# Residual and embedding rows by fours, and an earlier multiplication by the norm's weights, in the last stage of a decoder layer

## Chip, cores and metric

One core of a Trainium2 chip runs the whole kernel. The metric is the device time of one execution in microseconds (us). Runs of one kernel scatter by some 0.1%, so a change of less than 0.2% (4.3 us) counts here as no change.

## What is computed

One decoder layer on a residual stream of 1024 tokens by 1024 channels, all float32: a half-step feed-forward, a token mixer, a second half-step feed-forward, and a last stage that adds a gated embedding. The change touches the last stage alone:

```
def _rmsnorm(x, g):
    xf = x.astype(jnp.float32)
    y = xf * lax.rsqrt(jnp.mean(xf * xf, axis=-1, keepdims=True) + EPS)
    return (y * g.astype(jnp.float32)).astype(x.dtype)
...
        gate = jax.nn.sigmoid(_rmsnorm(h, ple_pre_g[i]) @ ple_w_gate[i])
        e = p[i] @ ple_w_proj[i]
        h = h + _rmsnorm(gate * e, ple_post_g[i])
```

## The kernel before

Tokens lie on the 128 partitions, so the 1024 tokens are eight **token blocks** t = 0 to 7, each 128 x 1024, cut into two halves of 512 channels. Every large product is done by Strassen's scheme (Winograd's form): both operands are cut into 2 x 2 blocks of 512, seven products of sums of blocks are formed in the order p1, p2, p5, p6, p3, p7, p4 (`ORDER`), and the result's blocks are read as they become complete: block 11 (t 0 to 3, first half) after p2, block 12 (t 0 to 3, second half) after p3, block 22 (t 4 to 7, second half) after p7, block 21 (t 4 to 7, first half) after p4. So t 0 to 3 are complete after the fifth product, t 4 to 7 after the seventh. Float32 accuracy comes from splitting each operand into a high and a low part (`split`: a cast on ScalarE, L147, then a subtraction on VectorE, L148) and three matmuls per step (`mm3`, L155 to L157). In the last stage a product has 4 token blocks x 4 steps x 3 = 48 matmuls of 128 x 512.

The left operand is held by `Seven`: seven tiles from the pool `X` (seven buffers of 16 KB per partition), filled as the token blocks of the normalized stream are transposed on TensorE (L232): op 0 and op 1 for p1 and p2, later op 2 to op 6 for p5, p6, p3, p7, p4 (`sums`, L207 to L218; the tile `rest` holds two of its terms). The right operand, the weights `ple_w_gate`, is loaded by `Rows` (L522) into the pool `raw` (six buffers), summed there (L151), and split into the pool `wt` (four buffers). `closing` ends the stage before: for each token block it computes the residual (L730), writes it to memory as `h3` (L731), and normalizes it (L178) for the transposes. The pools `f` (`full`, eleven tiles of 4 KB per partition) and `hf` (`half`, four of 2 KB) hold the rest.

`ple_final` (L1169 ff.) is called for each token block and half as a block of the gate product completes. It loads the half row of the embedding `e` (L1178, 256 KB), takes the sigmoid of the product (ScalarE, L1179), multiplies by e (VectorE, L1180) and sums the squares (ScalarE, L168). GpSimd computes the scale r = (mean + eps)^-0.5 of the row (L174 for the half that comes first; L162 and L163 with the second). For the half that completes the row it then loads the residual row h3 (L1185, 512 KB) and, for both halves, multiplies by r and by the norm's weights (`scaled`, L178), adds the residual (L151) and stores the result (L1191). The weights themselves are loaded once, when the first block arrives (L182).

All these loads and stores are issued by SyncE (SP) on one queue. The order of instructions on each engine is not written by hand: the framework's scheduler sets it from the program, together with the small work queue `later`, and each engine then runs its list strictly in that order. A tile whose pool is full takes the buffer that comes free, and its first writer waits for the last reader there.

Of the kernel before, what the change touches and what calls it, by code (L numbers as in the profile page):

```python
# [13 lines left out]
P = 128  # L14
# [69 lines left out]
def layer_kernel(ctx: ExitStack, tc: tile.TileContext, a: dict, out: bass.AP):  # L84
# [24 lines left out]
    def raw(shape, dt=F32):  # L109

        return rawp.tile([P, *shape], dt, name="raw", tag="raw")
# [5 lines left out]
    def half():  # L117

        return hfp.tile([P, HT], F32, name="hf", tag="hf")
# [39 lines left out]
    def rsqrt(src, scale, offset=EPS):  # L159

        ms, r = scalar_tile(), scalar_tile()
        nc.gpsimd.tensor_scalar(ms, src, scale, offset, op0=ALU.mult, op1=ALU.add)  # L162
        nc.gpsimd.tensor_tensor(r, ms, nhalf, op=ALU.pow)  # L163
        return r

    def squares(src, junk):
        ss = scalar_tile()
        nc.scalar.activation(junk, src, AF.Square, accum_out=ss)  # L168
        return ss

    def mean_part(src, junk, scale, offset):

        out = scalar_tile()
        nc.gpsimd.tensor_scalar(out, squares(src, junk), scale, offset, op0=ALU.mult, op1=ALU.add)  # L174
        return out
# [4 lines left out]
    def gain(vec):  # L180
        g = full()
        nc.sync.dma_start(g, vec.partition_broadcast(P))  # L182
        return g
# [322 lines left out]
    class Rows:  # L506
# [27 lines left out]
            make = from_stored(block, put, sums) if stored else from_blocks(block, put)  # L534
            self.right = Right(lambda i: make(i, state, (False, False)), list(range(7)), 1)

        def run(self, left, outs, last):
            for i, (name, place, fresh) in enumerate(ORDER):
                if i == 6:
                    last()  # L540
                left.need(i)
                o = self.right.get(i)
                for t in range(4):
                    if i == 2:
                        later.flush(t + 6 if t < 3 else None)
                    s = left.op[i]
                    if fresh:
                        outs[t].b[place] = bank()
                    cols = slice(t * P, (t + 1) * P)
                    for k in range(4):  # L550
                        oh = o[k // 2]
                        mm3(
                            outs[t].b[place], (s[:, 0, k, cols], s[:, 1, k, cols]),
                            (oh[:, 0, k % 2, :], oh[:, 1, k % 2, :]), fresh and k == 0, k == 3,
                        )
                    outs[t].read(name)
                    later.allow(2.7)
# [606 lines left out]
    )  # L1164


    m, parts, gains = {}, {}, []

    def ple_final(t, half_, part):  # L1169
        if not gains:  # L1170
            gains.append(gain(a["ple_post_g"][0]))
        g_ple = gains[0]
        h = slice(half_ * HT, (half_ + 1) * HT)
        if t not in m:
            m[t] = full()
        mt = m[t]
        e = half()
        nc.sync.dma_start(e, e_d[t][:, h])  # L1178
        nc.scalar.activation(mt[:, h], part, AF.Sigmoid)  # L1179
        nc.vector.tensor_tensor(mt[:, h], mt[:, h], e, op=ALU.mult)  # L1180
        if half_ != (1 if t < 4 else 0):
            parts[t] = mean_part(mt[:, h], e, 1.0 / D, EPS)
            return
        hp = raw([D])
        nc.sync.dma_start(hp, h3_d[t])  # L1185
        r = rsqrt(squares(mt[:, h], e), 1.0 / D, parts[t])
        for j in range(2):
            hj = slice(j * HT, (j + 1) * HT)
            scaled(mt[:, hj], mt[:, hj], r, g_ple[:, hj])
            add(hp[:, hj], hp[:, hj], mt[:, hj])  # L1190
            nc.sync.dma_start(out[0, t * P:(t + 1) * P, hj], hp[:, hj])  # L1191

    ple_rows.run(left, token_out(ple_final, m), lambda: None)


# [27 lines left out]
```

## Time and profile before

| | us |
|---|---|
| median of 3 runs | 2148.37 (2146.13 to 2148.41) |
| the profiled execution | 2153.78 |
| its span, first to last instruction | 2151.7 |
| last matmul of the stage before ends | 2033.7 |
| last matmul of the last stage ends | 2133.7 |
| busy in the span: TensorE (PE), VectorE (DVE), ScalarE (ACT), GpSimd (POOL) | 2070.9, 1472.0, 939.9, 141.0 |

In the profile PE is the matmul side of TensorE and PEld its weight load; PEclk is the clock that was granted to TensorE as a share of full speed. Busy time counts instructions that run. In a timeline the start of each instruction is the sound number: durations are given a little long where one instruction follows another at once (a VectorE operation of 128 x 512 reads 0.68 and starts 0.60 after the one before).

### The profile page before, as it was taken

The numbers are of one execution on the slowest core, as the hardware profiler recorded it, in microseconds if no ns is written. First come the engines' busy times: TensorE is split into PE (matmuls) and PEld (weight loads), VectorE is DVE, ScalarE is ACT, GpSimd is POOL, SyncE is SP. The second block draws the span as 40 slices with busy tenths as digits, with TensorE's granted clock in tenths as the row PEclk, the third lists the DMA queues.
The fourth block names the chain that finished last, engine by engine and source line by source line (L and its number), as shares of the span: only waits on it lengthen the run. The fifth ranks groups of instructions, "written<-read, shape, count | busy, mean of one in ns | idle before, by whom it ended". The sixth has DMA issues, their size and how long they took to land. (4 is left out here: it accounts for less than half of the span.)

```text
span 2151.7 us, 25497 instructions
## 1 busy us (share of the span) xinstructions
PE 2070.9 (96%) x9228; PEld 1712.7 (80%) x9228; DVE 1472.0 (68%) x1773; ACT 939.9 (44%) x1360; POOL 141.0 (7%) x212
## 2 busy tenths in 40 slices
PE   7999999999999799999999999989999999999986
PEld 6888888888887688888787887778888888888765
DVE  6866666677566887567576758886666667545687
ACT  7533333344435543334455535643333334444553
POOL 2000000000021110000000002300000000002112
PEclk9999999999999899999999999999999999999988
DMA  8454545399768236445389986635454547764635
GB/s 287 128 171 157 176 142 184 129 340 384 298 221 320 69 100 193 158 142 177 128 282 340 324 233 204 195 112 188 146 186 136 172 149 272 231 197 175 225 118 195
DMA packets 301486, 429.52 MB, mean 200 GB/s; under 512 B 19888, under 2 KB 176560, under 8 KB 301360
## 3 DMA queue, kind: packets, MB, share of 16 engines
q1 hardware_dynamic: 300272, 425.80, 58.3%
q0 software_dynamic: 1088, 2.10, 0.6%
q8 instruction: 72, 1.18, 0.2%
q14 instruction: 54, 0.44, 0.1%
HBM read 290.72 MB, written 137.10 MB: 199 GB/s over the span
## 5 line engine op out<-in xcount | busy, mean ns | idle before, releaser
L155 PE MATMUL ps<-X,wt 128*128 128x512 f32 x1904 | 743.0, 391 | 4.1 <-DVE f L345 2.4
L156 PE MATMUL ps<-X,wt 128*128 128x512 f32 x1904 | 743.2, 390 | 0.9 <-DVE X L148 0.9
L157 PE MATMUL ps<-X,wt 128*128 128x512 f32 x1904 | 741.8, 390 | 0.0
L148 DVE TENSOR_TENSOR wt<-raw,wt 128x1024 fp32r<-128x1024 f32 x282 | 343.5, 1220 | 235.0 <-ACT wt L147 234.9
L155 PEld LDWEIGHTS ps<-X,wt 128*128 128x128 f32 x1904 | 359.3, 189 | 79.3 <-DVE f L345 2.8
L156 PEld LDWEIGHTS ps<-X,wt 128*128 128x128 f32 x1904 | 359.2, 189 | 76.0 <-DVE X L148 1.8
L157 PEld LDWEIGHTS ps<-X,wt 128*128 128x128 f32 x1904 | 358.8, 188 | 74.7
L147 ACT CAST wt<-raw 128x1024 fp32r<-128x1024 f32 x282 | 295.5, 1050 | 268.7 <-PE ps L157 129.2
L148 DVE TENSOR_TENSOR X<-raw,X 128x1024 fp32r<-128x1024 f32 (+1 forms) x201 | 224.0, 1145 | 113.6 <-ACT X L147 113.1
L147 ACT CAST X<-raw 128x1024 fp32r<-128x1024 f32 (+1 forms) x201 | 192.1, 993 | 156.2 <-PE ps L157 66.6
L156 PE MATMUL ps<-X 128*128 128x512 f32 x616 | 241.5, 392 | 0.3 <-DVE X L148 0.3
L155 PE MATMUL ps<-X 128*128 128x512 f32 x616 | 237.4, 391 | 3.7 <-ACT X L147 2.6
L157 PE MATMUL ps<-X 128*128 128x512 f32 x616 | 240.2, 391 | 0.0
L151 DVE TENSOR_TENSOR raw<-raw 128x1024 f32<-128x1024 f32 x136 | 165.8, 1221 | 15.4 <-DMA raw<-in_w_in_dram 5.5
L155 PEld LDWEIGHTS ps<-X 128*128 128x128 f32 x616 | 116.1, 189 | 28.6 <-ACT X L147 3.0
L156 PEld LDWEIGHTS ps<-X 128*128 128x128 f32 x616 | 116.4, 189 | 24.7 <-DVE X L148 0.8
L156 PE MATMUL ps<-wt,X 128*128 128x512 f32 x336 | 133.8, 398 | 1.8 <-DVE wt L148 1.8
L157 PEld LDWEIGHTS ps<-X 128*128 128x128 f32 x616 | 116.4, 189 | 24.0
L155 PE MATMUL ps<-wt,X 128*128 128x512 f32 x336 | 132.1, 401 | 1.2 <-DVE f L345 1.2
L157 PE MATMUL ps<-wt,X 128*128 128x512 f32 x336 | 133.0, 396 | 0.0
L340 ACT ACTIVATE f<-ps 128x512 f32<-128x512 f32 x88 | 52.6, 598 | 122.5 <-PE ps L157 122.3
L338 ACT ACTIVATE f<-ps 128x512 f32<-128x512 f32 x88 | 52.0, 597 | 109.4 <-PE ps L157 109.4
(136 smaller groups left out, 1856.9 us busy)
## 6 DMA issues: line engine op xcount, KB each, us to landing
raw<-ffn_s SPq DMA_DIRECT2D x70, 512.0 KB, 5.2
raw<-in_ffn_w_gate_dram SPq DMA_DIRECT2D x96, 256.0 KB, 3.4
raw<-in_ffn_w_up_dram SPq DMA_DIRECT2D x96, 256.0 KB, 4.1
f<-in_ffn_w_down_dram SPq DMA_DIRECT2D x44, 512.0 KB, 4.6
ffn_s<-hf SPq DMA_DIRECT2D x88, 256.0 KB, 3.4
ffn_t<-hf SPq DMA_DIRECT2D x88, 256.0 KB, 4.3
raw<-ffn_t SPq DMA_DIRECT2D x40, 512.0 KB, 5.2
ffn_s<-f SPq DMA_DIRECT2D x66, 256.0 KB, 2.1
```

The source lines that it names most:

```text
L147: nc.scalar.copy(hi, src)
L148: e.tensor_tensor(lo, src, hi.bitcast(F32), op=ALU.subtract)
L151: e.tensor_tensor(dst, u, v, op=ALU.add)
L155: nc.tensor.matmul(ps, wl[1], wr[0], start=first, stop=False, skip_group_check=True)
L156: nc.tensor.matmul(ps, wl[0], wr[1], start=False, stop=False, skip_group_check=True)
L157: nc.tensor.matmul(ps, wl[0], wr[0], start=False, stop=last, skip_group_check=True)
L338: nc.scalar.activation(at("22"), y, AF.Copy, scale=-1.0)
L340: nc.scalar.activation(at("12"), x, AF.Copy, scale=-1.0)
```

## The change

`ple_final` no longer loads anything. A function `beside`, called once per product from `Rows.run`, loads the norm's weights and all eight embedding rows (two `X` tiles of four rows each) ahead of p6, and the residual rows of t 0 to 3 ahead of p3 and of t 4 to 7 ahead of p7 (an `X` tile each). Each row is its own load of 512 KB. The sigmoid of block 11 is taken at once, and everything behind it is kept back in `gated_steps` until the rows are there. Behind the multiplication by e, the half row is multiplied in place by the norm's weights; when r is there, one operation per half row multiplies by r and adds the residual in its `X` tile, from where it is stored.

```
-        def run(self, left, outs, last):
+        def run(self, left, outs, last, beside=lambda i: None):
...
                 o = self.right.get(i)
+                beside(i)
                 for t in range(4):
...
-    m, parts, gains = {}, {}, []
+    m, parts, gains, e, h = {}, {}, [], {}, {}
+
+    def rows_of(src, dst, ts):
+        tile4 = X([4, D], F32)
+        for n, t in enumerate(ts):
+            dst[t] = tile4[:, n]
+            nc.sync.dma_start(dst[t], src[t])
+
+    def beside(i):
+        if i == 3:
+            gains.append(gain(a["ple_post_g"][0]))
+            rows_of(e_d, e, range(4))
+            rows_of(e_d, e, range(4, 8))
+        if i in (4, 5):
+            rows_of(h3_d, h, range(4 * i - 16, 4 * i - 12))
...
-        e = half()
-        nc.sync.dma_start(e, e_d[t][:, h])
-        nc.scalar.activation(mt[:, h], part, AF.Sigmoid)
-        nc.vector.tensor_tensor(mt[:, h], mt[:, h], e, op=ALU.mult)
-        if half_ != (1 if t < 4 else 0):
-            parts[t] = mean_part(mt[:, h], e, 1.0 / D, EPS)
-            return
-        hp = raw([D])
-        nc.sync.dma_start(hp, h3_d[t])
-        r = rsqrt(squares(mt[:, h], e), 1.0 / D, parts[t])
-        for j in range(2):
-            hj = slice(j * HT, (j + 1) * HT)
-            scaled(mt[:, hj], mt[:, hj], r, g_ple[:, hj])
-            add(hp[:, hj], hp[:, hj], mt[:, hj])
-            nc.sync.dma_start(out[0, t * P:(t + 1) * P, hj], hp[:, hj])
...
+        nc.scalar.activation(mt[:, cols], part, AF.Sigmoid)
+
+        def gated():
+            nc.vector.tensor_tensor(mt[:, cols], mt[:, cols], e[t][:, cols], op=ALU.mult)
+            if half_ != (1 if t < 4 else 0):
+                parts[t] = mean_part(mt[:, cols], half(), 1.0 / D, EPS)
+            else:
+                r = rsqrt(squares(mt[:, cols], half()), 1.0 / D, parts[t])
+            nc.vector.tensor_tensor(mt[:, cols], mt[:, cols], gains[0][:, cols], op=ALU.mult)
+            if half_ != (1 if t < 4 else 0):
+                return
+            for j in range(2):
+                hj = slice(j * HT, (j + 1) * HT)
+                nc.vector.scalar_tensor_tensor(h[t][:, hj], mt[:, hj], r, h[t][:, hj], op0=ALU.mult, op1=ALU.add)
+                nc.sync.dma_start(out[0, t * P:(t + 1) * P, hj], h[t][:, hj])
+
+        gated_steps.append(gated)
+        if e and (t >= 4 or half_ == 0 or len(h) > t):
+            while gated_steps:
+                gated_steps.pop(0)()
```

In the changed kernel the three VectorE lines are L1192 (times e), L1197 (times the norm's weights) and L1202 (times r, plus residual); the row loads are L1174, the stores L1203. Every engine's list is the same as before up to the start of the last stage. Three places behind it, as the lists stand (line, operation, output <- inputs with tile numbers, shape):

VectorE, start of the last stage, up to the normalization of token block 7 (`raw_15308`), which its transposes need. `X_15324` is `rest`; `X_15327`, `X_15330` are op 2 and op 6; `X_15630` is op 3 (in the change `X_15600`), `X_15708` is op 4; the `raw` sums with `raw_15557` are weights of p6 and p7. Before:

```order
L730 SCALAR_TENSOR_TENSOR f_14327<-f_14327,sc_15311,raw_15308 128x1024
L214 SCALAR_TENSOR_TENSOR f_14804<-f_14804,X_15324 128x512
L215 TENSOR_TENSOR f_14804<-f_14804,X_15324 128x512
L148 TENSOR_TENSOR X_15630<-X_15324,X_15630 128x4x128
L151 TENSOR_TENSOR raw_15435<-raw_15435,raw_15557 128x1024
L151 TENSOR_TENSOR f_15346<-f_15346,ps_15451 128x512
L151 TENSOR_TENSOR raw_15439<-raw_15439,raw_15557 128x1024
L151 TENSOR_TENSOR f_15370<-f_15370,ps_15475 128x512
L148 TENSOR_TENSOR X_15327<-X_15324,X_15327 128x4x128
L148 TENSOR_TENSOR X_15330<-ps_15424,X_15330 128x4x128
L148 TENSOR_TENSOR X_15708<-f_14804,X_15708 128x4x128
L178 SCALAR_TENSOR_TENSOR raw_15308<-f_14327,sc_15354,f_14075 128x1024
```

And now:

```order
L731 SCALAR_TENSOR_TENSOR f_14327<-f_14327,sc_15311,raw_15308 128x1024
L207 TENSOR_TENSOR X_15324<-ps_15424,X_15324 128x4x128
L214 SCALAR_TENSOR_TENSOR f_14804<-f_14804,X_15324 128x512
L215 TENSOR_TENSOR f_14804<-f_14804,X_15324 128x512
L148 TENSOR_TENSOR X_15600<-X_15324,X_15600 128x4x128
L151 TENSOR_TENSOR f_15346<-f_15346,ps_15451 128x512
L151 TENSOR_TENSOR f_15370<-f_15370,ps_15466 128x512
L148 TENSOR_TENSOR X_15327<-X_15324,X_15327 128x4x128
L178 SCALAR_TENSOR_TENSOR raw_15308<-f_14327,sc_15354,f_14075 128x1024
L148 TENSOR_TENSOR X_15330<-ps_15424,X_15330 128x4x128
```

The two weight sums, the op 4 part and the op 6 part now stand behind the normalization (L207, which stood ahead of L730, stands behind L731); two more parts of op 4 and op 5 that stood ahead of L730 have gone behind as well, because op 4 and op 5 now wait for buffers.

SP's queue, the same stretch. Before:

```order
L522 DMA raw_15441<-in_ple_w_gate_dram 128x2x512
L731 DMA h3_6_103<-f_14316 128x1024
L1178 DMA hf_15467<-e_0_105 128x512
L1178 DMA hf_15489<-e_1_106 128x512
L1178 DMA hf_15527<-e_2_107 128x512
L1178 DMA hf_15549<-e_3_108 128x512
L522 DMA raw_15557<-in_ple_w_gate_dram 128x2x512
L182 DMA f_15465<-in_ple_post_g_dram 128x1024
L731 DMA h3_7_104<-f_14327 128x1024
L522 DMA raw_15559<-in_ple_w_gate_dram 128x2x512
```

And now (three embedding rows, t 0 to 2, stand between `raw_15441` and the first row shown):

```order
L732 DMA h3_6_103<-f_14316 128x1024
L1174 DMA X_15628<-e_3_108 128x1024
L1174 DMA X_15633<-e_4_109 128x1024
L1174 DMA X_15633<-e_5_110 128x1024
L1174 DMA X_15633<-e_6_111 128x1024
L1174 DMA X_15633<-e_7_112 128x1024
L522 DMA raw_15527<-in_ple_w_gate_dram 128x2x512
L732 DMA h3_7_104<-f_14327 128x1024
L522 DMA raw_15529<-in_ple_w_gate_dram 128x2x512
```

All eight embedding rows now stand ahead of the weights of p6 (`raw_15527`, `raw_15529`; before `raw_15557`, `raw_15559`). Farther on, the residual rows of t 0 to 3 stand directly behind them, then p4's weights, then the norm's weights, then the residual rows of t 4 to 7, then all sixteen stores.

VectorE, the end of its list. Before:

```order
L178 SCALAR_TENSOR_TENSOR f_15582<-f_15582,sc_15975,f_15465 128x512 x2
L1180 TENSOR_TENSOR f_15627<-f_15627,hf_16056 128x512
L178 SCALAR_TENSOR_TENSOR f_15597<-f_15597,sc_16005,f_15465 128x512
L151 TENSOR_TENSOR raw_15970<-raw_15970,f_15582 128x512
L178 SCALAR_TENSOR_TENSOR f_15597<-f_15597,sc_16005,f_15465 128x512
L151 TENSOR_TENSOR raw_15970<-raw_15970,f_15582 128x512
L178 SCALAR_TENSOR_TENSOR f_15612<-f_15612,sc_16035,f_15465 128x512 x2
L151 TENSOR_TENSOR raw_16000<-raw_16000,f_15597 128x512
L178 SCALAR_TENSOR_TENSOR f_15627<-f_15627,sc_16065,f_15465 128x512 x2
L151 TENSOR_TENSOR raw_16000<-raw_16000,f_15597 128x512
L151 TENSOR_TENSOR raw_16030<-raw_16030,f_15612 128x512 x2
L151 TENSOR_TENSOR raw_16060<-raw_16060,f_15627 128x512 x2
```

And now:

```order
L1202 SCALAR_TENSOR_TENSOR X_15869<-f_15552,sc_15976,X_15869 128x512 x2
L1197 TENSOR_TENSOR f_15567<-f_15567,f_15626 128x512
L1202 SCALAR_TENSOR_TENSOR X_15869<-f_15567,sc_16002,X_15869 128x512
L1197 TENSOR_TENSOR f_15582<-f_15582,f_15626 128x512
L1192 TENSOR_TENSOR f_15597<-f_15597,X_15633 128x512
L1202 SCALAR_TENSOR_TENSOR X_15869<-f_15582,sc_16028,X_15869 128x512
L1202 SCALAR_TENSOR_TENSOR X_15869<-f_15567,sc_16002,X_15869 128x512
L1202 SCALAR_TENSOR_TENSOR X_15869<-f_15582,sc_16028,X_15869 128x512
L1197 TENSOR_TENSOR f_15597<-f_15597,f_15626 128x512
L1202 SCALAR_TENSOR_TENSOR X_15869<-f_15597,sc_16054,X_15869 128x512 x2
```

Behind the last multiplication by e (L1180 before, L1192 now) stood 14 operations, and stand 6.

## Rows read from the trace of the kernel before

**Rows 1.** The page, part 1: busy time, share, instructions.

```profile
PE 2070.9 (96%) x9228; PEld 1712.7 (80%) x9228; DVE 1472.0 (68%) x1773; ACT 939.9 (44%) x1360; POOL 141.0 (7%) x212
```

**Rows 2.** Busy time by stretch: PE, PEld, DVE, ACT, POOL, PEclk, DMA share, GB/s.

```profile
2033.70:2069.20 35.50, 23.09 (x105) 18.57 (x105) 31.68 (x41) 19.80 (x35) 10.09 (x11) 0.87 0.40 134
2069.20:2133.70 64.50, 62.65 (x266) 50.87 (x264) 46.60 (x65) 33.38 (x64) 10.44 (x18) 0.97 0.52 164
2133.70:2151.70 18.00, 0.07 (x1) 0.00 (x0) 12.11 (x19) 2.65 (x7) 4.60 (x7) 0.63 0.37 141
```

**Rows 3.** Timeline of PE: start, us, line, operation, [idle before it <- who ended it].

```profile
2052.26 1.27 PE L232 MATMUL ps<-ident,raw 128*128 128x128 f32 x8 [2.59 <-DVE raw L178]
2053.18 0.78 PE L155 MATMUL ps<-wt,X 128*128 128x512 f32 x1
2067.60 1.97 PE L232 MATMUL ps<-ident,raw 128*128 128x128 f32 x8 [7.17 <-DVE raw L178]
2069.22 0.77 PE L155 MATMUL ps<-wt,X 128*128 128x512 f32 x1
2070.22 0.63 PE L157 MATMUL ps<-wt,X 128*128 128x512 f32 x1
2079.49 1.07 PE L155 MATMUL ps<-wt,X 128*128 128x512 f32 x4
2122.12 0.50 PE L155 MATMUL ps<-wt,X 128*128 128x512 f32 x1 [1.22 <-DVE f L345]
2123.26 0.49 PE L156 MATMUL ps<-wt,X 128*128 128x512 f32 x1 [0.63 <-DVE wt L148]
```

**Rows 4.** Timeline of DVE at the start of the last stage.

```profile
2052.73 0.67 DVE L148 TENSOR_TENSOR X<-f,X 128x512 fp32r<-128x512 f32 x1
2058.01 1.27 DVE L730 SCALAR_TENSOR_TENSOR f<-f,sc,raw 128x1024 f32<-128x1024 f32 x1
2061.01 1.21 DVE L151 TENSOR_TENSOR raw<-raw 128x1024 f32<-128x1024 f32 x1
2066.27 1.27 DVE L178 SCALAR_TENSOR_TENSOR raw<-f,sc 128x1024 f32<-128x1024 f32 x1
```

**Rows 5.** Timeline of POOL: the scale of block 7, and two small operations later.

```profile
2060.54 1.72 POOL L162 TENSOR_SCALAR sc<-sc 128x1 f32<-128x1 f32 x1 [7.93 <-DVE f L215]
2062.35 0.55 POOL L163 TENSOR_TENSOR sc<-sc,nhalf 128x1 f32<-128x1 f32 x1
2126.18 3.22 POOL L174 TENSOR_SCALAR sc<-sc 128x1 f32<-128x1 f32 x2 [5.99 <-ACT hf L168]
2129.97 0.19 POOL L174 TENSOR_SCALAR sc<-sc 128x1 f32<-128x1 f32 x1 [0.57 <-ACT hf L168]
```

**Rows 6.** Chain of waits that ended last, from 2120 on: start, us, what.

```profile
2129.91 7.77 DMA hf<-e
2142.21 1.40 DVE f L178 x2
2146.74 1.81 DVE raw L151 x3
```

**Rows 7.** Timelines: DVE at the end, SP (queue of loads and stores) at two places.

```profile
2139.06 0.68 DVE L1180 TENSOR_TENSOR f<-f,hf 128x512 f32<-128x512 f32 x1
2145.46 3.08 DVE L151 TENSOR_TENSOR raw<-raw,f 128x512 f32<-128x512 f32 x5
2118.50 0.38 SPq L522 DMA_DIRECT2D raw<-in_ple_w_gate_dram  x1
2044.24 0.37 SPq L522 DMA_DIRECT2D raw<-in_ple_w_gate_dram  x1
```

**Rows 8.** DMA issues from 2005 on (KB each, median us to landing), and one stretch.

```profile
raw<-in_ple_w_gate_dram SPq DMA_DIRECT2D x12, 512.0 KB, 4.3
f<-in_ple_post_g_dram SPq DMA_DIRECT2D x1, 512.0 KB, 5.5
2010.00:2020.00 10.00, 10.00 (x46) 8.29 (x45) 8.75 (x10) 5.15 (x6) 0.13 (x1) 1.00 0.96 313
```

More of the change, by code (lines that the diff above doesn't have):

```diff
@@ L1164, in layer_kernel @@
     )
-    m, parts, gains = {}, {}, []
+    m, parts, gains, e, h = {}, {}, [], {}, {}
[11 more added lines that the diff above has]
+            rows_of(h3_d, h, range(4 * i - 16, 4 * i - 12))
     def ple_final(t, half_, part):
[L1170 to L1173, printed above, removed]
+        cols = slice(half_ * HT, (half_ + 1) * HT)
         if t not in m:
@@ L1176, in ple_final @@
         mt = m[t]
-        e = half()
-        nc.sync.dma_start(e, e_d[t][:, h])
-        nc.scalar.activation(mt[:, h], part, AF.Sigmoid)
-        nc.vector.tensor_tensor(mt[:, h], mt[:, h], e, op=ALU.mult)
-        if half_ != (1 if t < 4 else 0):
-            parts[t] = mean_part(mt[:, h], e, 1.0 / D, EPS)
-            return
-        hp = raw([D])
-        nc.sync.dma_start(hp, h3_d[t])
-        r = rsqrt(squares(mt[:, h], e), 1.0 / D, parts[t])
-        for j in range(2):
-            hj = slice(j * HT, (j + 1) * HT)
-            scaled(mt[:, hj], mt[:, hj], r, g_ple[:, hj])
-            add(hp[:, hj], hp[:, hj], mt[:, hj])
-            nc.sync.dma_start(out[0, t * P:(t + 1) * P, hj], hp[:, hj])
-    ple_rows.run(left, token_out(ple_final, m), lambda: None)
+        nc.scalar.activation(mt[:, cols], part, AF.Sigmoid)
[16 more added lines that the diff above has]
+                gated_steps.pop(0)()
+    gated_steps = []
+    ple_rows.run(left, token_out(ple_final, m), lambda: None, beside)
 _INS = [
```

## The prediction

> **What bounds the kernel now.** The page's first part shows TensorE busy for 96% of the span [rows 1]: time can be won only where TensorE waits, or behind its last matmul. The engines' lists are unchanged up to 2033.7 us, so I read the last 118 us alone, cut into three stretches [rows 2]. In the first TensorE is busy 23.1 of 35.5 us and VectorE 31.7: TensorE waits for VectorE. In the second TensorE is busy 62.7 of 64.5. The third, 18.0 us, is the tail behind the last matmul. So the stage holds 12.4, 1.9 and 18.0 us without matmuls.
>
> The timeline of TensorE then shows which work ends each wait [rows 3]. The transposes of token blocks 6 and 7 wait 2.59 and 7.17 us for the normalization L178 on VectorE, and p4 waits 1.22 and 0.63 us for its weights. In the tail, the chain of waits spends 7.77 us on the last half rows of e, and then walks through VectorE's operations on four token blocks to the last stores [rows 6].
>
> All terms come from one execution of 2153.78 us, whose span is 2151.7; 2.1 us lie around it. It is 5.4 us above the median of 2148.37. I subtract the terms from the median. A difference under 0.2%, or 4.3 us, is about what a measurement of this kernel cannot tell from no change.
>
> **The start of the stage.** VectorE works back to back here; an operation of 128 x 512 takes 0.60 us from start to start and a weight sum of 128 x 1024 about 1.14 ([rows 4] read 0.67 and 1.21, overlap included). Of the work ahead of block 7's normalization, three parts of op 4 and op 5, one of op 6 and two weight sums move behind it: 4 x 0.60 + 2 x 1.14 = 4.7 us. L178 would start at 2066.27 - 4.7 = 2061.6 [rows 4]. Its other input is r, ready at 2062.90 now [rows 5]. L730, from which r is computed, comes 3 x 0.60 = 1.8 us earlier (two parts and L207 leave the place ahead of it), so r comes at 2061.1 and does not hold L178. TensorE's wait shrinks from 7.17 to 2.5 us, about the 2.59 ahead of block 6's transposes. After that wait the first matmul came 0.92 us behind the start of the transposes, after the long one 1.62; and after the long one some ten matmuls ran at 0.43 us a piece instead of 0.23, after the short one seven (the lower clock level: 0.63 long where a full-speed one reads 0.39, [rows 3]). That is another 0.7 + 3 x 0.2 = 1.3. So p2 ends 4.7 + 1.3 = 5.9 us earlier, and the first matmuls of p6, at 2079.5 + 0.2 now [rows 3], would be wanted at 2073.7.
>
> Part of that is given back. What left the path still has to be done before p6's weights are ready. From L178's end at 2062.8 to the subtraction of the first of them stand eleven operations of 0.60 and four of 1.14, or 11.2 us, and the subtraction takes 1.2: 2075.2, or 1.5 us late. Net at p5 and p6: **4.4 us**. The bounds are 0 (the normalization is held by something else) and 5.9 (no wait for the weights), and with no slow matmuls at all 1.4 more.
>
> **The loads.** The embedding rows are 8 x 512 KB where 16 x 256 KB were, the residual rows 8 x 512 KB as before, the norm's weights one load: no bytes are saved. What changes is the place in SP's queue. The eight e rows stand ahead of p6's weights; their price is in the rivals. The norm's weights go to a buffer that comes free only with the op 5 parts, which wait for p5's end, at about 2087 by this walk; with the 5.5 us that this load took [rows 8] and as much again for the residual rows queued ahead of it they are there by 2098. Four multiplications and half of p7's weights are queued behind them on VectorE; p7 wants these at about 2106. The operations take 3 us, so 5 us of slack cover the load; if the cover went, TensorE would wait at p7 for what the load is late beyond it.
>
> **p4's weights.** Their load is issued at 2118.50 now [rows 7], because its buffer was lent to a residual row. Residual rows no longer use that pool, so the load goes out near 2087, 29 us before use. Both waits ahead of p4 go: **1.85 us** (bounds 0 and 1.85).
>
> **VectorE's sum** does not change: per half row two multiplications and an addition, 48 operations, become two multiplications and a combined one, 48 again. A change that seems to save an operation saves none; it moves one ahead of r.
>
> **The tail.** Now 18.0 us from the last matmul to the end. The 7.77 us on e go, for the rows were loaded long before: 10.2 left as an upper bound. From below: sigmoid about 0.75; the last block's multiplication by e to its first use of r 3.15 (2139.06 to 2142.21, [rows 6, 7]); two combined operations 1.4, as the two L178 there; and 3.1 from the last VectorE operation to the end (2145.46 + 3.08 to 2151.7, [rows 7]): 8.4. VectorE's list has three operations of other blocks and a wait for r ahead of the last multiplication by e, and three behind it, so I add 1.5 and take 9.9. Gain **8.1 us** (bounds 7.8 and 9.6).
>
> One rule of the Trainium skill speaks against this part. First the row: on GpSimd two operations took 3.22 us where one took 0.19 later [rows 5]; VectorE ran four operations with two operands from SBUF meanwhile, and GpSimd went on when they ended. The multiplication by the norm's weights is such an operation, put exactly between the squares and r. The page "SBUF — State Buffer" ("Who interferes with whom") calls the port pair of VectorE and GpSimd an exclusive lock: the later one waits for the whole instruction. By that rule the last r comes 0.6 us later, or up to 3.0 where four operations queue; by the chain at the end now, none of it, since the 3.15 was measured with VectorE busy. The sum goes by the 3.15 of the rows, and the range keeps 3.0 as the row's 3.22 less 0.19.
>
> **Sum.** 4.4 + 1.85 + 8.1 = 14.4 us: 2148.4 - 14.4 = **2134.0 us**.
>
> **Rivals.**
> 1. *The start is not won.* Block 7's normalization waits for r or a load and TensorE starts again where it does now. For it: GpSimd needed 1.72 us for an operation of 0.2 [rows 5], and r would be early by only half a microsecond. Against it: r's inputs move with it. Time: 2134.0 + 4.4 = 2138.4. If VectorE's tail queue is longer too, 2142.
> 2. *Rows ahead of weights.* From 2044.2 [rows 7] to p6's first weights, SP is to issue ten loads and stores of 512 KB where it issues six now, four of them half as large: with these weights 5.8 MB. VectorE reaches the sum that needs them four operations behind L178, at 2062.8 + 2.4 = 2065.2, with everything for p6 queued behind it. At the 313 GB/s of a stretch with its DMA engines 96% busy [rows 8] they land at 2062.6, in time. At the 134 GB/s that this stretch moves on average [rows 2] they would land at 2087.3, 22.1 us late: 2156, **slower**. From 163 GB/s downward (14.4 us late) all is given back. Against it: 134 is a mean with the engines 40% busy, so the demand, not the queue, set it. The page "DMA: Bandwidth & Descriptors" ("Queues, rings and completion order") of the Trainium skill says that each engine takes the descriptors of one queue in order, so that late weights wait for every row ahead. No row shows here what eight rows in front cost.
> 3. *The multiplication does not run beside the squares.* It writes in place what ScalarE still reads for the squares, so it must follow them. Then it stands beside GpSimd's work only, and if it is not hidden there the end is 0.6 us later: 2134.6. It is inside the forecast.
>
> **Chances.** Forecast (2130 to 2137, rival 3 included) 0.62; the start not won, 2138 to 2142, 0.18; better than 2130 (no slow matmuls, VectorE on time) 0.04; rows somewhat late, up to 2144, 0.04; rows late by the whole gain, within 4.3 us of now, 0.07; later still, 0.05. The first four are faster by over 0.2%: 0.88. The range 2129.5 to 2142 takes in the bounds 3.0 and 4.4 of the unknown terms and leaves out about 2 in 10.
>
> **What would show it.** Right: in the profile after, the wait ahead of block 7's transposes falls to 2 to 3 us; none stands ahead of p4; a short one for p6's weights appears inside p5; VectorE waits for no e in the tail, which falls to 8.5 to 10.2 us. Wrong: VectorE idle for `raw` weights or for the norm's weights, with TensorE waiting at p6 or p7; or a 7 us wait at block 7 as before; or a tail in which VectorE waits for r more than 2 us in all.

## The result and the profile after

The changed kernel took **2132.84 us** (median of 4 runs, 2130.59 to 2133.69), the kernel before 2147.25 us beside it (4 runs, 2146.08 to 2148.41): a ratio of **0.9931, 95% interval 0.9914 to 0.9948**. That is 14.4 us, or 0.5 to 0.9%. The forecast was 2134.0 us. A second measurement of the same kernel, the last experiment below, gave 2135.38 us beside 2146.84 and 0.9940 (0.9927 to 0.9954): 11.5 us.

The profiled execution of the change took 2130.59 us, its span is 2128.9. Its last stage begins 7.1 us earlier than in the profiled execution of before, in which nothing ahead of the stage differs; that is drift between executions. So both stages are counted here from the transposes of block 4 (2034.59 us before, 2027.46 after) to the end of the span.

| us from block 4's transposes | before | after | earlier by |
|---|---|---|---|
| block 6's transposes start | 17.67 | 17.01 | 0.66 |
| block 7's transposes start | 33.01 | 27.84 | 5.17 |
| first matmuls of p6 | 45.1 | 38.7 | 6.4 |
| last matmul ends | 99.0 | 90.2 | 8.8 |
| end of the span | 117.1 | 101.4 | 15.7 |

The page's first line, and the windows of the three stretches, cut at the matching places (us; PE, PEld, DVE, ACT, POOL busy and their instructions; granted clock; DMA share; GB/s):

```profile
PE 2065.3 (97%) x9228; PEld 1708.6 (80%) x9228; DVE 1472.2 (69%) x1773; ACT 938.1 (44%) x1360; POOL 152.6 (7%) x212
```

```profile
2026.80:2056.90 30.10, 22.89 (x105) 18.54 (x106) 26.94 (x36) 17.83 (x32) 8.50 (x11) 0.92 0.65 244
2056.90:2117.70 60.80, 60.80 (x264) 49.97 (x263) 55.31 (x79) 35.92 (x71) 21.44 (x20) 0.98 0.38 139
2117.70:2128.90 11.20, 0.12 (x1) 0.00 (x0) 7.49 (x12) 1.32 (x3) 4.88 (x5) 0.63 0.48 187
```

VectorE has as many instructions as before [rows 1], and the same busy time within 0.2 us. Against [rows 2] the stretches without matmuls are 7.2, 0 and 11.2 us where they were 12.4, 1.9 and 18.0. VectorE's work has moved into the middle stretch: 55.3 us there instead of 46.6.

The timeline of TensorE, beside [rows 3]:

```profile
2044.47 1.09 PE L232 MATMUL ps<-ident,raw 128*128 128x128 f32 x8 [2.00 <-DVE raw L178]
2055.30 1.54 PE L232 MATMUL ps<-ident,raw 128*128 128x128 f32 x8 [2.67 <-DVE raw L178]
2065.98 1.07 PE L155 MATMUL ps<-wt,X 128*128 128x512 f32 x4
```

The wait ahead of block 7 is 2.67 us where it was 7.17, p6 starts without one, and no row between here and the end carries a wait: both of p4's are gone.

VectorE's timeline, beside [rows 4] and [rows 7]:

```profile
2053.88 1.28 DVE L178 SCALAR_TENSOR_TENSOR raw<-f,sc 128x1024 f32<-128x1024 f32 x1
2066.22 1.22 DVE L148 TENSOR_TENSOR wt<-raw,wt 128x1024 fp32r<-128x1024 f32 x1
2084.07 1.23 DVE L151 TENSOR_TENSOR raw<-raw 128x1024 f32<-128x1024 f32 x1 [3.71 <-DMA raw<-in_ple_w_gate_dram]
2117.29 1.43 DVE L1202 SCALAR_TENSOR_TENSOR X<-f,sc,X 128x512 f32<-128x512 f32 x2 [0.80 <-POOL sc L163]
2120.51 0.68 DVE L1192 TENSOR_TENSOR f<-f,X 128x512 f32<-128x512 f32 x1
2124.49 1.42 DVE L1202 SCALAR_TENSOR_TENSOR X<-f,sc,X 128x512 f32<-128x512 f32 x2 [0.72 <-POOL sc L163]
```

From 2084 us to the end VectorE is never idle for longer than 0.8 us. It waits for no embedding row; it waits for r 0.80 us just ahead of the last matmul's end (2117.7) and 0.72 us in the tail. New is the 3.71 us for p4's weights.

The chain of waits at the end, beside [rows 6], now passes through the squares and GpSimd instead of a load:

```profile
2120.58 0.61 DVE f L1192
2121.28 0.63 ACT hf L168
2122.10 1.72 POOL sc L162
...
2124.49 0.75 DVE X L1202
```

GpSimd's timeline, beside [rows 5], and SP's, beside [rows 7]:

```profile
2111.51 4.45 POOL L174 TENSOR_SCALAR sc<-sc 128x1 f32<-128x1 f32 x2 [1.30 <-ACT hf L168]
2122.10 1.72 POOL L162 TENSOR_SCALAR sc<-sc 128x1 f32<-128x1 f32 x1 [1.72 <-ACT hf L168]
```

```profile
2039.48 5.11 SPq L1174 DMA_DIRECT2D X<-e  x5
2045.60 0.38 SPq L522 DMA_DIRECT2D raw<-in_ple_w_gate_dram  x1
...
2074.62 1.74 SPq L1174 DMA_DIRECT2D X<-h  x4
2076.85 1.52 SPq L522 DMA_DIRECT2D raw<-in_ple_w_gate_dram  x2
```

p6's first weights are issued at 2045.60, behind the eight embedding rows, and p4's at 2076.85, behind four residual rows.

### The profile page after: what moved, and what is told of

Read it like the earlier page. It is cut to its first block, busy times and chain, and to the rows that moved or that the text cites. A ratio compares the mean times of both kernels' runs of the same rounds, so it can differ in the third digit from the quotient of the medians.

```text
span 2128.9 us, 25453 instructions
## 1 busy us (share of the span) xinstructions
PE 2065.3 (97%) x9228; PEld 1708.6 (80%) x9228; DVE 1472.2 (69%) x1773; ACT 938.1 (44%) x1360; POOL 152.6 (7%) x212
## 5 line engine op out<-in xcount | busy, mean ns | idle before, releaser
L155 PE MATMUL ps<-X,wt 128*128 128x512 f32 x1904 | 742.1, 390 | 1.7 <-DVE wt L148 1.7
L155 PEld LDWEIGHTS ps<-X,wt 128*128 128x128 f32 x1904 | 358.8, 188 | 76.5 <-DVE wt L148 2.2
L155 PE MATMUL ps<-X 128*128 128x512 f32 x616 | 237.4, 391 | 3.1 <-ACT X L147 1.9
L155 PEld LDWEIGHTS ps<-X 128*128 128x128 f32 x616 | 116.2, 189 | 28.1 <-ACT X L147 2.3
L155 PE MATMUL ps<-wt,X 128*128 128x512 f32 x336 | 131.7, 398 | 0.0
```

The lines of the kernel that those rows point to most:

```text
L155: nc.tensor.matmul(ps, wl[1], wr[0], start=first, stop=False, skip_group_check=True)
```

## Experiments

Diffs are against the changed kernel, except where another base is named. Every experiment was compared with the kernel before on its own chip. Times in the stage are from one profiled execution each, counted as above. "Tail" is from the end of the last matmul.

| kernel | ratio to before (95%) | median, us | last matmul | tail | stage |
|---|---|---|---|---|---|
| rows alone (e1) | 0.9957 (0.9942 to 0.9972) | 2136.19 | 89.3 | 14.7 | 104.0 |
| weights alone (e2) | 0.9978 (0.9969 to 0.9987) | 2142.97 | 97.3 | 12.6 | 109.9 |
| embedding rows and weights (e3) | 0.9954 (0.9939 to 0.9969) | 2135.90 | 90.7 | 12.7 | 103.5 |
| buffers held, no loads (e4) | 0.9992 (0.9983 to 1.0002) | 2144.66 | 96.8 | 17.0 | 113.8 |
| one GpSimd operation (e5) | 0.9933 (0.9918 to 0.9948) | 2133.03 | 90.6 | 11.4 | 102.0 |
| norm's weights early (e6) | 0.9926 (0.9911 to 0.9940) | 2131.17 | 90.9 | 10.4 | 101.3 |
| e rows twice (e7) | 0.9943 (0.9926 to 0.9959) | 2134.52 | 91.0 | 12.3 | 103.3 |
| e5 and e6 (e8) | 0.9933 (0.9918 to 0.9948) | 2132.52 | 91.8 | 9.9 | 101.7 |
| r from half a row (e9) | 0.9938 (0.9925 to 0.9952) | 2134.09 | 90.8 | 11.5 | 102.3 |
| e6 once more (e10) | 0.9932 (0.9920 to 0.9945) | 2132.15 | 90.7 | 10.4 | 101.1 |
| the change once more (e11) | 0.9940 (0.9927 to 0.9954) | 2135.38 | 91.8 | 11.2 | 103.0 |

**Rows alone (e1).** The multiplication by the norm's weights goes back behind r:

```diff
-            nc.vector.tensor_tensor(mt[:, cols], mt[:, cols], gains[0][:, cols], op=ALU.mult)
...
-                nc.vector.scalar_tensor_tensor(h[t][:, hj], mt[:, hj], r, h[t][:, hj], op0=ALU.mult, op1=ALU.add)
+                scaled(mt[:, hj], mt[:, hj], r, gains[0][:, hj])
+                add(h[t][:, hj], h[t][:, hj], mt[:, hj])
```

> The loads by fours as in the change, but the multiplication by the norm's weights stays behind r, as before the change (four operations per block behind r instead of two). Counted from the transposes of token block 4, the kernel before needs 99.0 us to its last matmul and 18.1 us behind it, the change 90.2 and 11.2. Theory (the loads and the buffers they hold win nearly all): the wait ahead of block 7 is 2 to 3 us, no wait ahead of p4, the last matmul ends at 90 to 91, and the tail is 1.4 us longer than in the change, 12 to 13: 102.5 to 104 in all. Rival (the multiplication ahead of r carries a good part of the tail): a tail of 14.5 or more. Rival (the multiplication between squares and r locks GpSimd out and costs what it saves): a tail of 10.5 to 11.5.

The start is won as in the change, and p4's wait is gone. The tail is 14.7 us, the first rival's case and not the theory's 12 to 13, so the order of the two multiplications is worth 3.5 us there. Windows from the last matmul to VectorE's end, of this kernel and of the change (columns as above):

```profile
2119.40:2131.10 11.70, 0.16 (x1) 0.00 (x0) 10.90 (x17) 1.58 (x5) 5.83 (x6) 0.63 0.35 134
```

```profile
2117.70:2125.90 8.20, 0.12 (x1) 0.00 (x0) 7.48 (x12) 1.32 (x3) 4.88 (x5) 0.68 0.50 192
```

In both VectorE is busy all but 0.7 to 0.8 us: 17 operations are left at the last matmul here, 12 in the change. Both kernels have 48 operations for the half rows. But here 32 of them can run only behind r (a scaling and an addition for each of 16 half rows), in the change 16.

**Weights alone (e2).** Against the kernel before: the weights are multiplied in ahead of r, all rows are loaded as before.

```diff
+            nc.vector.tensor_tensor(mt[:, h], mt[:, h], g_ple[:, h], op=ALU.mult)
...
-            scaled(mt[:, hj], mt[:, hj], r, g_ple[:, hj])
-            add(hp[:, hj], hp[:, hj], mt[:, hj])
+            nc.vector.scalar_tensor_tensor(hp[:, hj], mt[:, hj], r, hp[:, hj], op0=ALU.mult, op1=ALU.add)
```

> The multiplication by the norm's weights ahead of r as in the change, but every load as before it. Theory (loads win nearly all): the wait ahead of block 7 is 7 us as before, about 1.9 us of waiting stay ahead of p4, VectorE still waits for the last half rows of e in the tail, and only 1 to 3 us go from the tail: 114 to 116.5 us in all, where 117.1 is before and 101.4 the change. Rival (the multiplication carries the tail): a tail of 13 or less, 112 or less in all.

The start is not touched: block 7's transposes start 33.0 us into the stage, as before (they wait 8.77 us, since TensorE came to the wait earlier). The tail is 5.5 us shorter than before, the rival's case, and p4's waits shrink to 0.51. VectorE waits for no embedding row in this tail, though each half row is loaded as before, where it lost 3.53 and 1.19 us in the kernel before:

```profile
2135.25 0.69 DVE L1180 TENSOR_TENSOR f<-f,hf 128x512 f32<-128x512 f32 x1 [3.53 <-DMA hf<-e]
2137.13 0.69 DVE L1180 TENSOR_TENSOR f<-f,hf 128x512 f32<-128x512 f32 x1 [1.19 <-DMA hf<-e]
```

So the early rows are not the only way to take these waits away. The parts do not add up: rows alone 13.1 us of the stage, weights alone 7.3, together 15.7, because both shorten the same tail and the same waits at p4.

**Embedding rows and weights (e3).** The residual rows go back to the pool of p4's weights:

```diff
-        if i in (4, 5):
-            rows_of(h3_d, h, range(4 * i - 16, 4 * i - 12))
...
+            h[t] = raw([D])
+            nc.sync.dma_start(h[t], h3_d[t])
```

> The embedding rows by fours and the multiplication ahead of r, as in the change; the residual rows one by one into the pool of the weights, as before it. Theory (two X buffers held by e free the start, the residual rows' buffers set p4's weights): the wait ahead of block 7 is 2 to 3 us; 1 to 2 us of waiting stay ahead of p4; the tail is that of the change, 11 to 12: 103 to 104.5 us in all. Rival (the start needs all four X tiles, or p4's weights were late for another reason): 7 us ahead of block 7, or no wait ahead of p4.

No wait at p4, where the theory had 1 to 2 us, though residual rows take buffers of that pool again. So that alone does not make p4's wait. The residual rows in operand memory are worth some 1.5 us of tail (12.7 for 11.2).

**Buffers held, no loads (e4).** Against the kernel before: two buffers of operand memory are taken where the embedding rows take them, and released later; nothing is loaded there.

```diff
+            for _ in range(2):
+                held.append(X([4, D], F32))
+                nc.gpsimd.memset(held[-1][:, 0, 0:1], 0.0)
```

> The kernel before, with two X buffers taken ahead of p6 and held to p4, and nothing loaded into them (one column is set to zero and read back on GpSimd). Every load and every operation of the stage as before. Theory (the start is won because op 4 and op 5 find no buffer, and their work leaves VectorE's list ahead of block 7; the two weight sums stay ahead of it here): the wait ahead of block 7 falls by 2.4 us plus what the shorter wait saves in slow matmuls, to 4.5 to 5.2; the last matmul ends 2 to 4 us earlier than before; p4's wait and the tail of 18 stay: 113 to 115.5 us in all, where 117.1 is before. Rival (the start is won by the loads): 7 us ahead of block 7 and 116.5 to 118 in all.

Timeline of TensorE, block 7's transposes:

```profile
2059.63 1.94 PE L232 MATMUL ps<-ident,raw 128*128 128x128 f32 x8 [6.46 <-DVE raw L178]
```

They start 2.5 us earlier than before (30.5 for 33.0) with nothing loaded into these buffers: the lack of buffers pushes four half-row operations of VectorE behind block 7's normalization, and that is where this part of the gain comes from. The two weight sums stay ahead of it here. The idle time fell less than the theory put it, since TensorE also came to the wait 1.8 us earlier. The time alone does not separate this kernel from the one before.

**One GpSimd operation (e5).** The lock tested:

```diff
-                parts[t] = mean_part(mt[:, cols], half(), 1.0 / D, EPS)
+                parts[t] = scalar_tile()
+                nc.scalar.activation(parts[t], squares(mt[:, cols], half()), AF.Copy, scale=1.0 / D, bias=EPS)
...
-                r = rsqrt(squares(mt[:, cols], half()), 1.0 / D, parts[t])
+                ms, r = scalar_tile(), scalar_tile()
+                ss = squares(mt[:, cols], half())
+                nc.scalar.activation(ms, ss, AF.Identity, scale=1.0 / D, bias=parts[t])
+                nc.gpsimd.tensor_tensor(r, ms, nhalf, op=ALU.pow)
```

> Of the three small operations that lead to a block's r in the last stage, the two ahead of the power go from GpSimd to ScalarE (the half's mean as a Copy with scale and bias, the row's mean as an Identity with the half's as bias), so GpSimd has one operation for each block where it had three. Nothing is left out. The stage is counted from the transposes of block 4 to the end of the span; the change takes 101.4 us there, 11.2 of them behind the last matmul. Theory: GpSimd's small operations stand still beside VectorE's operations with two operands in operand memory (4.45 us for two, 1.72 for one in the trace of the change), and that makes r late; with one operation in place of three VectorE waits for r less than 0.8 us in all (1.5 in the change), the tail is 9.7 to 10.7 us and the stage 100 to 101, 0.5 to 1.5 us less than the change in the time too. Rival: VectorE's own list, without a break from 2084 us on, sets the tail, and r is late by the list and not by the lock: tail 11.0 to 11.5, stage 101.2 to 101.8. A second rival: the power alone, met by the same operations, stands as long as the three did, and ScalarE's steps come on top: tail 11.5 to 13.

VectorE's timeline:

```profile
2119.69 1.41 DVE L1206 SCALAR_TENSOR_TENSOR X<-f,sc,X 128x512 f32<-128x512 f32 x2 [0.44 <-POOL sc L1200]
2126.61 1.41 DVE L1206 SCALAR_TENSOR_TENSOR X<-f,sc,X 128x512 f32<-128x512 f32 x2 [0.44 <-POOL sc L1200]
```

GpSimd's, at the last block:

```profile
2124.79 1.78 POOL L1200 TENSOR_TENSOR sc<-sc,nhalf 128x1 f32<-128x1 f32 x1 [3.28 <-ACT sc L1199]
```

The waits for r shrink from 0.80 and 0.72 to 0.44 each, the tail does not (11.4), which is the first rival's range. But the one operation left stood 1.78 us at the last block, as one of the three did in the change (1.72): the lock has not gone from this run, so what it costs at the end is not shown.

**Norm's weights early (e6).**

```diff
-        if i == 3:
+        if i == 1:
             gains.append(gain(a["ple_post_g"][0]))
+        if i == 3:
```

> The norm's weights are asked for at the start of the stage (at p5 instead of p3's place in the list), so that their load goes out between the two loads of p6's weights, and four of the multiplications by them stand at the start of the stage on VectorE, ahead of p6's weights, where in the change they stand at 2084 us and later. Nothing is left out. Theory: VectorE's list, without a break from 2084 to 2126 us, sets when the last rows are ready, so four operations of 0.6 us less in it (2.4 us) bring the tail from 11.2 to 9 to 10 us; p6's first three matmuls need no result of VectorE and the other weights have slack, so the last matmul stays at 90.2 (within 0.5). Stage 99 to 100.4. Rival 1: the tail is set by the chain of the last block (its multiplication by e, squares, r), not by what is in front of it: tail 10.9 to 11.4, stage 101.1 to 101.7. Rival 2: the multiplications ahead of p6's weights make TensorE wait there: a wait of 1 to 3 us inside p5 or p6, last matmul 91 to 93.

Windows from the last matmul to VectorE's end:

```profile
2119.00:2126.40 7.40, 0.14 (x1) 0.00 (x0) 6.58 (x11) 2.01 (x5) 3.47 (x4) 0.68 0.51 197
```

The tail is 0.8 us shorter, not 1.2 to 2.2. Four operations left the list at 2087 us, but at the last matmul only one fewer is left than in the change: VectorE had caught up by then and waited 0.27 us for ScalarE at 2114.37 and 0.80 for r at 2117.07. The last matmul came 0.7 later, as block 6's transposes already did (17.67, as in before).

**Embedding rows twice (e7).** Rival 2 priced:

```diff
             rows_of(e_d, e, range(4, 8))
+            for t in range(NT):
+                nc.sync.dma_start(e[t], e_d[t])
```

> Every embedding row is loaded a second time into the same place, 8 x 512 KB more; three of the second copies stand in SP's queue ahead of p6's first weights, eight ahead of their second part. VectorE's list is partly in another order with it. Nothing is left out, one load is done twice. This prices rows ahead of weights, the mechanism of the rival that ended slower: the change has about 2.6 us to spare at p6's weights. Theory: late rows in the queue are late weights; three more rows are 1.6 MB, 5 us at the 313 GB/s of the full stretch, so p6's weights land after they are wanted, TensorE waits 2 to 8 us for them, and the time is 2 to 8 us longer than the change's. Rival: the queue has room, the rows are hidden once more: no wait at p6, the time within 1 us of the change.

TensorE waits nowhere behind block 7's 2.67 us, so the theory's wait did not come; the stage is 1.9 us longer, 1.1 of it in the tail. The landing time of p6's first weights, in the view of the tile `raw` over the stretch of their issue, here and in the change:

```profile
DMA to landing us min/median/max: 10.2/10.2/10.2
```

```profile
DMA to landing us min/median/max: 9.3/9.3/9.3
```

They land 4.0 us later in the stage (issued 3.1 later, 0.9 slower). In the change they land at 2054.9 and VectorE asks for them at 2057.48, so 2.6 us are to spare; these 4.0 would have made VectorE late by 1.4. But its list has another order here: the sums of these weights stand at 2062.39, 33.2 us into the stage, where the change has them at 30.0, and so nothing waited. What a wait at p6 would have cost stays open. Rows ahead of the weights do make them late, here by 1.4 us on that reckoning where the rival needed 14.4.

**Both (e8).** The edits of e5 and e6 together.

> The one operation on GpSimd for each block and the early norm's weights together. Nothing is left out. If the lock and VectorE's list each hold a part of the tail: tail 8.3 to 9.3 us, stage 98 to 99.5, time 2 to 3 us under the change's. If both act on the same wait: no better than the better of the two alone, tail 9 to 10. If neither: 11.2, stage 101.4.

The shortest tail, 9.9 us, in the range given if both edits act on the same wait, and no better time: TensorE ended 1.6 us later than in the change. Its wait at block 7 was 4.16 us, and from there to the last matmul it took 63.4 us for 62.4; the last experiment shows the same course.

**r from half a row (e9).** The squares of the second half stay, but r does not use them.

```diff
-                r = rsqrt(squares(mt[:, cols], half()), 1.0 / D, parts[t])
+                squares(mt[:, cols], half())
+                r = rsqrt(parts[t], 1.0, EPS)
```

> r of a row is computed from the mean of its first half alone; the squares of the second half are still taken, but nothing waits for them. That is the part of the computation that changes: the last norm uses half a row. Every engine has as many operations as in the change, the same small ones on GpSimd included. The stage of the change is 101.4 us with a tail of 11.2. Theory: the way from the last multiplication by e over the squares and GpSimd to r (3.98 us in the change, 3.15 in the sum of the prediction) is what holds VectorE at the end, since the lock alone and a shorter list moved the tail by less than 1 us each: without it VectorE does not wait for r, and what is left is the sigmoid (0.7), one multiplication (0.6), some seven operations (4.5) and 3.0 behind VectorE, a tail of 8.8 to 9.8 and a stage of 98.9 to 100.2. Rival: VectorE's list is full anyway, and r comes in its shadow: tail 10.6 to 11.3, stage 100.8 to 101.6.

Windows from the last matmul to VectorE's end, then GpSimd's timeline:

```profile
2121.20:2129.70 8.50, 0.17 (x1) 0.00 (x0) 8.06 (x13) 2.04 (x5) 4.01 (x6) 0.82 0.45 174
```

```profile
2116.23 3.64 POOL L174 TENSOR_SCALAR sc<-sc 128x1 f32<-128x1 f32 x2 [2.11 <-ACT hf L168]
```

The way over the second half's squares is gone and the tail is 11.5: the rival's case (a little above its range). VectorE has 13 operations left behind the last matmul and is idle 0.44 us. r was still late by 1.26 us at 2120.80, ahead of this window, because GpSimd stood 3.64 us beside VectorE's multiplications. So this run, too, has waits for r, 1.70 us in all.

**The early weights and the change once more (e10, e11).** The two kernels unchanged, side by side.

> The kernel with the early norm's weights once more, beside the change itself on the same chip and in more rounds. Nothing is left out. If its shorter tail (10.4 us for 11.2) is a gain, it is 0.5 to 2 us below the change here; if the earlier difference of 1.7 us was drift between executions, the two agree within 0.5 us.

> The change itself, as the yardstick for the kernel with the early norm's weights. Nothing is left out. Both theories: 2131.5 to 2134.5 us, a tail of 10.9 to 11.6 and a wait of 2.6 to 2.8 us ahead of block 7's transposes.

The early weights are 1.7 us below the change in the first comparison and 3.2 in this one, and the tail is 10.4 again where the change has 11.2 again. The intervals overlap, so the time alone does not separate them. The tail rows do, by 0.8 us, but in the first pair the whole stage is the same (101.3 and 101.4 us). It is the version I would keep. The change itself came out above the range expected of it, with a wait of 4.16 us at block 7:

```profile
2060.63 1.94 PE L232 MATMUL ps<-ident,raw 128*128 128x128 f32 x8 [4.16 <-DVE raw L178]
```

Windows of TensorE from block 6's transposes to block 7's and 10.8 us on, in the first profile of the change and in this one:

```profile
2044.50:2055.30 10.80, 8.13 (x32) 6.40 (x33) 10.80 (x15) 6.27 (x10) 2.06 (x3) 0.84 0.99 402
2055.30:2066.10 10.80, 10.80 (x45) 9.06 (x46) 10.80 (x15) 6.78 (x13) 3.96 (x2) 0.84 0.15 51
```

```profile
2049.90:2060.60 10.70, 6.57 (x32) 5.23 (x32) 10.70 (x15) 6.27 (x10) 2.07 (x3) 0.94 0.95 384
2060.60:2071.40 10.80, 10.77 (x40) 9.06 (x41) 10.80 (x15) 6.08 (x12) 3.56 (x2) 0.74 0.14 50
```

Block 7 comes 10.8 us behind block 6 in both, because VectorE sets it. In e11 TensorE did its 32 matmuls at a higher granted clock (0.94 for 0.84), waited longer, and then ran at the lower one (0.74 for 0.84): 40 matmuls where the other did 45. From block 7's transposes to the last matmul it took 63.4 us for 62.4. The same program thus has a stage of 101.4 or 103.0 us. The longer wait alone is not what costs: in e10 block 7 waited 4.19 us too, but the slow stretch of the clock lay ahead of block 6 there (0.81 from 2037 to 2046 us, 1.00 from then to block 7), 44 matmuls ran in the 10.7 us behind the wait, at 0.84, and from block 7's transposes to the last matmul it took 62.4.

## Why the prediction was right, and where it was not

**What bounds the kernel.** As put. The three stretches were the places, and VectorE at the start and the embedding rows in the tail were what ended the waits. At p4 VectorE's list had a part that was put down to the loads.

**The start: 4.7 us.** Held. From block 6's transposes to block 7's it took 15.3 us before, 10.8 in the change and in e11: 4.5 to 4.6. The term of slow matmuls (1.3) held in the first profile: from block 7's transposes to p6's first matmuls 12.1 us before, 10.9 after. In e11 it was 0.15 us, and the wait of 4.16 lies outside the 2 to 3 that were to show the step right. Of the order, e4 shows one half: with the buffers alone, L178 starts 11.6 us behind block 6's transposes, 14.0 before and 9.4 in the change. The other half, the two weight sums, moves only where the embedding rows stand ahead of p6's weights. These land at 2054.9 in the change, behind L178 at 2053.88; that the sums move for this reason is argued, not shown.

**Given back at p6: 1.5 us.** This failed: there is no such wait. The step took all matmuls of p6 to need VectorE's subtraction. The subtraction came at 2066.22, 0.2 us behind p6's first matmuls at 2065.98. But the row shows L155 four times in a run, of which three are p6's: the first of the three products needs only the high part of the weights, which ScalarE writes (cast at 2062.67). The early matmuls were of that kind, and 35 matmuls of p5 stood between them and the rest of p6, whose first group has no L155 of its own left:

```profile
2074.82 0.39 PE L156 MATMUL ps<-wt,X 128*128 128x512 f32 x1
```

So the low part was wanted 8.6 us later than the step had it (2074.8 for 2066.2), and was there 7.4 us ahead. Counted from block 6's transposes, p6's first matmuls came 5.7 us earlier in the change and 4.7 in e11, where the step had 4.4.

**p4: 1.85 us.** The waits went, and what remains of the gain of TensorE (8.1 us from block 6's transposes to the last matmul, 7.2 in e11) is 2.4 to 2.5. The term counted the idle time alone. Rows of the kernel before, with the two waits of [rows 3] between the last two:

```profile
2112.11 0.38 SPq L522 DMA_DIRECT2D raw<-in_ple_w_gate_dram  x1
2116.51 1.23 DVE L151 TENSOR_TENSOR raw<-raw 128x1024 f32<-128x1024 f32 x1 [0.48 <-DMA raw<-in_ple_w_gate_dram]
2121.98 1.22 DVE L148 TENSOR_TENSOR wt<-raw,wt 128x1024 fp32r<-128x1024 f32 x1
2120.29 0.61 PE L155 MATMUL ps<-wt,X 128*128 128x512 f32 x2
2123.59 0.39 PE L157 MATMUL ps<-wt,X 128*128 128x512 f32 x1
```

From 2120.29 to 2123.59 four matmuls start, 3.3 us where a run of four takes 0.9: 2.4 us lost.

The reason was misread in part. The load of 2118.50 is the second of p4's two; its sum starts only at 2123.12, and TensorE goes on at 2123.26 without it. The 0.63 us ended with the subtraction for the first load, which was issued at 2112.11 and there by 2116.51; this subtraction stood 3.1 us behind its cast, in VectorE's list. The 1.22 us carry L345 [rows 3], VectorE's reading of p7's result. So VectorE's list held p4 as well as the load did. e3 takes buffers of the pool again and has no wait. What the runs show is that the waits shrink as p4's first load goes out earlier: 77.5 us into the stage before (1.85 us of waiting), 75.3 in e4 (2.03), 74.0 in e2 (0.51), 69.0 in e3 and 49.4 in the change (none).

Nor did the load go unnoticed in the change: it stood behind four residual rows, took 7.3 us, and VectorE waited 3.71 for it. TensorE was not reached, since p4 begins some 22 us later. That is rival 2's mechanism at another place. VectorE's list, though, runs from there to the end without a wait above 0.8 us, so these 3.71 us are in its backlog. What they cost at the end is not tested; e6, with 2.4 us of work less behind them, had a tail 0.8 us shorter.

**The tail: 8.1 us, to 9.9.** This was mis-sized: it fell by 6.9, to 11.2, twice, outside the 8.5 to 10.2 that were to show it right. Two more rows of the change:

```profile
2117.86 0.60 ACT L1189 ACTIVATE f<-ps 128x512 f32<-128x512 f32 x1 [0.61 <-PE ps L157]
2123.10 0.68 DVE L1197 TENSOR_TENSOR f<-f 128x512 f32<-128x512 f32 x1
```

In the step's own terms, from the last matmul's end at 2117.7: the sigmoid is done after 0.76 us (0.75 in the step); from there to the last multiplication by e 2.05 (1.5); from this to the first use of r 3.98 (3.15); the last two operations 1.4 (1.4); behind them 3.0 (3.1). Two terms were too small: the one for other blocks' work in VectorE's list, and the way to r, on which one operation of GpSimd stood 1.72 us.

What the runs show in place of the one chain is VectorE's backlog. With the last matmul 12 operations are left, 7.5 us; 0.7 of waiting and the 3.0 behind them make 11.2. The count carries over: 17 operations give 14.7 (e1), 14 give 12.6 and 12.7 (e2, e3), 13 give 12.3 and 11.5 (e7, e9), 12 give 11.4 in e5 too, 11 give 10.4 (e6, e10), 10 give 9.9 (e8), and the 3.0 stand behind VectorE in each. This is a count, not yet a cause: part of the backlog is itself waiting for r, and neither e9 nor e5, which were to take that away, is free of it.

Rival 3's order is the one that the trace has: the multiplication by the norm's weights (2123.10) follows the squares (2121.28) and ends before r is used at 2124.49, so at the last block it is hidden.

**The lock.** The rule of the Trainium skill that was weighed there ("SBUF — State Buffer", "Who interferes with whom") agrees with the rows in that small operations of GpSimd took 4.45 us for two, and 1.72 for one, beside VectorE's operations with two inputs in operand memory (SBUF), against 0.27 elsewhere. In one point the rows go further: GpSimd stood through a run of such operations and not through one alone, 8.32 us for two of its own in e6. The bound of 3.0 us was not reached: VectorE waited for r 0.72 us in the tail and 0.80 just ahead of it. What the lock costs at the end stays open. e5 took away 0.64 of these 1.52 us and the tail was no shorter, but it was not free of the lock.

**Rows ahead of weights.** Rival 2 did not decide. p6's weights landed 9.3 us after issue, where the same load took 3.8 before and the median was 4.3 [rows 8], which agrees with the ring order of the Trainium skill's page "DMA: Bandwidth & Descriptors" ("Queues, rings and completion order"). But the queue moved 402 GB/s there, not 134 and not 313.

**The count of operations.** "48 again" was right, and the sentence that an operation only moves ahead of r named the gain without pricing it: e1 puts it at 3.5 us of tail.

**The sum.** The terms 4.4, 1.85 and 8.1 became 4.7 to 5.7, 2.4 to 2.5 and 6.9: 14.1 to 15.0 us for 14.4. The errors cancelled: 0.9 to 1.9 too little ahead of the last matmul, 1.2 too much behind it. The time was right to 1.2 us partly for that reason; the second measurement was 1.4 us above the forecast.

## What to carry to other kernels

When one engine feeds the end of a kernel, count what is left in its list when the last matmul ends, and not only the chain of the last block; an edit that leaves the number of operations alone can still pay by moving them ahead of the late input. A lack of operand buffers can change the order that a scheduler finds, and that order can be worth some us (2.4 in e4) with no load moved. Before putting a wait down to a load, read in its row what ended it. Before pricing a wait for weights, see which part of them the first matmuls need.

## What the runs showed of the hardware

- Loads issued in a row from one queue moved 402 GB/s over 10.8 us of the change (from 2044.5) and 412 over the 10.0 inside them (from 2045.0), where the fastest stretch read before had 313.
- Two GpSimd operations on 128 x 1 took 8.32 us in e6 (2075.57 us), the longest seen. Their VectorE neighbours had two operands in operand memory throughout.
- The same program waited 2.67 or 4.16 us for the same event, with a granted clock, between its two levels (1.2 and 2.4 GHz), of 0.84 or 0.94 ahead of it. In e11 0.94 was followed by 0.74, and from block 7 on TensorE took 1.0 us more; in e10, after a wait of 4.19, 1.00 was followed by 0.84, and it took no more.
